# Batch normalisation on one core: four parameter vectors loaded as rows by ScalarE's queue and turned onto the partitions by VectorE

## Chip, cores, metric

One core of a Trainium2 chip. The time is device microseconds of one execution; "before" and "changed" are compared by the medians of their runs.

## The reference

```python
# x: (32, 256, 128, 128) float32; the four parameters: (256,) float32
def reference(x, gamma, beta, running_mean, running_var):
    eps = 1e-5
    mean = running_mean.reshape(1, -1, 1, 1)   # var, gamma, beta likewise
    # ...
    return gamma * (x - mean) / np.sqrt(var + eps) + beta
```

The input and the output are 537 MB each. The parameters are 1 KB each.

## The kernel before

The kernel puts channels on the 128 partitions. A tile is 128 channels of one image: 128 x 16384 floats, 64 KB on each partition, 8.39 MB in all; there are 64 of them and room for three. All large transfers go through SyncE's queue. Per tile VectorE does one multiply-add in place, with a scale and a shift per partition.

```python
NBUF = 3
# ...
    for i in range(NBUF):
        issue_load(i)                      # nc.sync.dma_start, 8.39 MB each

    def load_param(ap_1d):                 # channel j*128 + p goes to partition p, column j
        t = params.tile([P, NCB], mybir.dt.float32, tag=ap_1d.tensor.name)
        nc.gpsimd.dma_start(out=t, in_=ap_1d.rearrange("(j p) -> p j", p=P))
        return t

    var_t = load_param(running_var)        # ... gamma, beta, running_mean
    # ... scale = gamma / sqrt(var + eps), shift = beta - mean * scale, on 128x2
    K = NBUF - 1
    for b in range((NT + K - 1) // K):
        idxs = [i for i in range(K * b, K * b + K) if i < NT]
        for i in idxs:
            compute(i)                     # one multiply-add of 128x16384
        for i in idxs:
            store(i)                       # nc.sync.dma_start
        for i in idxs:
            issue_load(i + NBUF)
```

A parameter load in this form is 256 pieces of 4 bytes, because neighbouring channels lie on different partitions.

## Time and profile before

| Quantity | Value | Where it is read |
|---|---|---|
| Median of the three runs known at the prediction | 2491.8 us (2489.7 to 2493.3) | the runs |
| Mean rate of the transfers | 432 GB/s | page |
| VectorE busy | 23% | page |
| First multiply-add starts | 25.56 us | timeline |
| Store 0 issued, landed | 34.40 us, 82.9 us | timeline, chain |

First, the page of the kernel before. The digits are the busy share of the DMA engines in 40 slices, in tenths, and GB/s is what they moved in each; a line of the queue table gives packets, MB and the share of 16 engines' span.

```profile
DMA  9999999999999999999999999999999999999998
GB/s 414 429 438 433 433 429 437 436 430 431 435 436 433 428 437 436 434 428 436 433 437 428 435 435 435 426 437 436 435 427 435 436 438 426 434 437 436 432 431 378
...
q1 hardware_dynamic: 18432, 1073.75, 99.8%
q0 software_dynamic: 128, 0.00, 0.0%
```

The DMA engines have no free slice, so the time is bytes over rate. The rate is near the ceiling of 435 GB/s (bytes through the 16 ports of SBUF, the core's memory in which the tiles lie) that the Trainium skill, "DMA: Bandwidth & Descriptors", section "Where 436 GB/s comes from", gives for 16 engines, and the trace agrees with it: its packet records show a steady median of 2.418 us for a 64 KB packet, which is 27.1 GB/s per engine and 434 GB/s for 16. The same section says that between HBM (the chip's main memory) and SBUF a lower limit binds, some 358 GB/s per core; this program, on one core, moved 432 GB/s, so here the measurement decides. The parameters' queue has 128 packets and next to no share.

The start decides what the parameters can cost. This is the timeline of the kernel before: start in us, duration in us, engine and line, and in brackets the idle time before it and what ended it.

```profile
0.74 1.33 SPq L48 DMA_DIRECT2D t<-in_x_dram  x3
...
1.25 0.84 POOL L56 DMA_DIRECT2D t<-in_running_var_dram  x1 [0.81 <-PEq L133]
...
12.44 1.28 ACT L71 ACT_TABLE_LOAD   x1 [12.44 <-DMA t<-in_running_var_dram]
...
17.42 0.16 DVE L79 TENSOR_TENSOR scale_t<-t,tmp_t 128x2 f32<-128x2 f32 x1 [3.20 <-DMA t<-in_gamma_dram]
25.17 0.16 DVE L80 TENSOR_TENSOR tmp_t<-t,scale_t 128x2 f32<-128x2 f32 x1 [7.58 <-DMA t<-in_running_mean_dram]
...
25.56 8.81 DVE L86 TENSOR_SCALAR t<-t,scale_t,shift_t 128x16384 f32<-128x16384 f32 x1
34.40 19.06 SPq L97 DMA_DIRECT2D out_dram<-t  x2
44.28 8.81 DVE L86 TENSOR_SCALAR t<-t,scale_t,shift_t 128x16384 f32<-128x16384 f32 x1 [9.91 <-DMA t<-in_x_dram]
63.64 8.81 DVE L86 TENSOR_SCALAR t<-t,scale_t,shift_t 128x16384 f32<-128x16384 f32 x1 [10.55 <-DMA t<-in_x_dram]
82.93 0.34 SPq L48 DMA_DIRECT2D t<-in_x_dram  x1
```

The first multiply-add is released by running_mean at 25 us. But the store of its tile, issued at 34.40 us, waits in the same queue behind loads 1 and 2, whose multiply-adds can start only at 44.28 and 63.64 us. The merged chain of waits (start, duration, what ran) shows the next link:

```profile
34.40 48.51 DMA out_dram<-t
...
82.93 38.59 DMA t<-in_x_dram
```

Store 0 takes 48.5 us from issue to landing, though a tile needs only some 19.3 us of the DMA engines; the rest is time in the queue. The chain follows the multiply-add back to the parameters, but that piece of chain has slack that the view does not show: an earlier issue of store 0 would only wait longer in the queue.

The group of multiply-adds, with busy time, mean of one, and idle time before them:

```profile
L86 DVE TENSOR_SCALAR t<-t,scale_t,shift_t 128x16384 f32<-128x16384 f32 x64 | 564.0, 8812 | 1868.0 <-DMA t<-in_x_dram 1867.9
```

VectorE spends its idle time waiting for tiles.

### The profile page before, as it was taken

The numbers are of one execution on the slowest core, as the hardware profiler recorded it, in microseconds if no ns is written. First come the engines' busy times: TensorE is split into PE (matmuls) and PEld (weight loads), VectorE is DVE, ScalarE is ACT, GpSimd is POOL, SyncE is SP. The second block draws the span as 40 slices with busy tenths as digits, with TensorE's granted clock in tenths as the row PEclk, the third lists the DMA queues.
The fourth block names the chain that finished last, engine by engine and source line by source line (L and its number), as shares of the span: only waits on it lengthen the run. The fifth ranks groups of instructions, "written<-read, shape, count | busy, mean of one in ns | idle before, by whom it ended". The sixth has DMA issues, their size and how long they took to land.

```text
span 2488.1 us, 378 instructions
## 1 busy us (share of the span) xinstructions
DVE 564.7 (23%) x69; ACT 1.6 (0%) x2; POOL 3.2 (0%) x8
## 2 busy tenths in 40 slices
DVE  2122211222112221122212222121221212212121
ACT  0000000000000000000000000000000000000000
POOL 0000000000000000000000000000000000000000
DMA  9999999999999999999999999999999999999998
GB/s 414 429 438 433 433 429 437 436 430 431 435 436 433 428 437 436 434 428 436 433 437 428 435 435 435 426 437 436 435 427 435 436 438 426 434 437 436 432 431 378
DMA packets 18562, 1073.77 MB, mean 432 GB/s; under 512 B 2176, under 2 KB 2176, under 8 KB 2176
## 3 DMA queue, kind: packets, MB, share of 16 engines
q1 hardware_dynamic: 18432, 1073.75, 99.8%
q0 software_dynamic: 128, 0.00, 0.0%
q14 instruction: 2, 0.02, 0.0%
HBM read 536.88 MB, written 536.87 MB: 432 GB/s over the span
## 4 chain that ended last, share of the span: by engine, by line
DMA 51%; another core or an unknown queue 36%; DVE 11%; SPq 0%; issue 0%; POOL 0%; DVEq 0%; POOLq 0%; PEldq 0%
DMA t<-in_x_dram 48%; DVE t L86 11%; DMA out_dram<-t 2%; DMA t<-in_running_mean_dram 1%; SPq L97 0%; POOL t L56 0%; DVEq L86 0%; POOLq L133 0%; SPq L48 0%; DVE shift_t L81 0%; DVE tmp_t L80 0%; DVEq L80 0%; PEldq L133 0%
## 5 line engine op out<-in xcount | busy, mean ns | idle before, releaser
L86 DVE TENSOR_SCALAR t<-t,scale_t,shift_t 128x16384 f32<-128x16384 f32 x64 | 564.0, 8812 | 1868.0 <-DMA t<-in_x_dram 1867.9
L78 DVE RECIPROCAL tmp_t<-tmp_t 128x2 f32<-128x2 f32 x1 | 0.2, 166 | 13.2 <-ACT tmp_t L71 13.2
L80 DVE TENSOR_TENSOR tmp_t<-t,scale_t 128x2 f32<-128x2 f32 x1 | 0.2, 160 | 7.6 <-DMA t<-in_running_mean_dram 7.6
L71 ACT ACT_TABLE_LOAD x1 | 1.3, 1283 | 12.4 <-DMA t<-in_running_var_dram 12.4
L79 DVE TENSOR_TENSOR scale_t<-t,tmp_t 128x2 f32<-128x2 f32 x1 | 0.2, 160 | 3.2 <-DMA t<-in_gamma_dram 3.2
L56 POOL DMA_DIRECT2D t<-in_running_var_dram x1 | 0.8, 839 | 0.8 <-PEq L133 0.8
L56 POOL DMA_DIRECT2D t<-in_gamma_dram x1 | 0.7, 722 | 0.0
L56 POOL DMA_DIRECT2D t<-in_beta_dram x1 | 0.7, 722 | 0.0
L56 POOL DMA_DIRECT2D t<-in_running_mean_dram x1 | 0.7, 722 | 0.0
L71 ACT ACTIVATE tmp_t<-t,eps_t 128x2 f32<-128x2 f32 x1 | 0.3, 295 | 0.0
L65 DVE MEMSET eps_t<- 128x1 f32 x1 | 0.1, 59 | 0.8 <-PEq L122 0.8
L81 DVE TENSOR_TENSOR shift_t<-t,tmp_t 128x2 f32<-128x2 f32 x1 | 0.2, 160 | 0.0
L122 POOL MEMSET const-bfloat16-1.0<- 128x1 bf16 x1 | 0.1, 96 | 0.0
L122 POOL MEMSET const-uint8-127<- 128x1 uint8 x1 | 0.1, 94 | 0.0
L122 POOL MEMSET const-float32-0.0<- 128x1 f32 x1 | 0.1, 93 | 0.2 <-issue 0.2
L122 POOL MEMSET const-float32-1.0<- 128x1 f32 x1 | 0.1, 93 | 0.0
## 6 DMA issues: line engine op xcount, KB each, us to landing
t<-in_x_dram SPq DMA_DIRECT2D x64, 38.6
out_dram<-t SPq DMA_DIRECT2D x64, 49.9
t<-in_running_var_dram POOLq DMA_DIRECT2D x1, 1.0 KB, 11.1
t<-in_gamma_dram POOLq DMA_DIRECT2D x1, 1.0 KB, 15.2
t<-in_beta_dram POOLq DMA_DIRECT2D x1, 1.0 KB, 19.5
t<-in_running_mean_dram POOLq DMA_DIRECT2D x1, 1.0 KB, 21.6
```

Source lines behind the costliest of these rows:

```text
L56: nc.gpsimd.dma_start(out=t, in_=ap_1d.rearrange("(j p) -> p j", p=P))
L65: nc.vector.memset(eps_t, eps)
L71: nc.scalar.activation(out=tmp_t[:], in_=var_t[:], func=mybir.ActivationFunctionType.Sqrt, bias=eps_t[:], scale=1.0,)
L78: nc.vector.reciprocal(out=tmp_t[:], in_=tmp_t[:])
L79: nc.vector.tensor_mul(out=scale_t[:], in0=gamma_t[:], in1=tmp_t[:])
L80: nc.vector.tensor_mul(out=tmp_t[:], in0=mean_t[:], in1=scale_t[:])
L81: nc.vector.tensor_sub(out=shift_t[:], in0=beta_t[:], in1=tmp_t[:])
L86: nc.vector.tensor_scalar(out=t[:], in0=t[:], scalar1=scale_t[:, cb : cb + 1], scalar2=shift_t[:, cb : cb + 1], op0=mybir.AluOpType.mult, ...
L122: nc = _bacc.Bacc("TRN2", target_bir_lowering=False, num_devices=1)
```

## The change

The intent is to replace the four scattered loads by four contiguous rows, take GpSimd out of the kernel, and have the parameters earlier. The order of tiles and transfers on SyncE's queue is kept. VectorE turns 32x32 blocks and four copies move the pieces onto the 128 partitions. The changed kernel also has the line `ctx.enter_context(tc.manual_schedule())`, which the cut below leaves out.

```diff
-    def load_param(ap_1d):
-        t = params.tile([P, NCB], mybir.dt.float32, tag=ap_1d.tensor.name)
-        nc.gpsimd.dma_start(out=t, in_=ap_1d.rearrange("(j p) -> p j", p=P))
-        return t
+    rows = params.tile([B, C], f32, tag="rows")              # B = 32, C = 256
+    nc.vector.memset(rows, 0.0)
+    for r, ap in enumerate((running_var, gamma, beta, running_mean)):
+        nc.scalar.dma_start(out=rows[r : r + 1, :], in_=ap.rearrange("(o c) -> o c", o=1))
 # ... the three first loads of x follow here ...
+    turned = params.tile([B, C], f32, tag="turned")
+    nc.vector.transpose(out=turned[:], in_=rows[:])
+    par = params.tile([P, NCB, 4], f32, tag="par")
+    blocks = turned.rearrange("p (cb q r) -> p cb q r", cb=NCB, q=NQ)   # NQ = 4
+    for q in range(NQ):
+        nc.vector.tensor_copy(out=par[q * B : (q + 1) * B], in_=blocks[:, :, q, 0:4])
+    var_t, gamma_t, beta_t, mean_t = (par[:, :, r] for r in range(4))
 # ... the loop over tiles is rewritten with the same order of computes, stores and loads ...
```

More of the change, by code (lines that the diff above doesn't have):

```diff
@@ L7 @@
 from concourse._compat import with_exitstack
-SINGLE_QUEUE = True
 NBUF = 3
+GROUPS = [2] * 32
+AHEAD = 1
 @with_exitstack
@@ L26 @@
     eps = 1e-5
+    f32 = mybir.dt.float32
     N, C, H, W = x.shape
@@ L33 @@
     NT = N * NCB
+    B = 32
+    NQ = P // B
+    assert sum(GROUPS) == NT and max(GROUPS) <= NBUF
     params = ctx.enter_context(tc.tile_pool(name="params", bufs=1))
@@ L39, with load @@
     outr = out.rearrange("n (cb p) h w -> (n cb) p (h w)", p=P)
+    ctx.enter_context(tc.manual_schedule())
     tiles = {}
-    loads = {}
-    def issue_load(i):
-        if i >= NT:
-            return
-        t = data.tile([P, HW], mybir.dt.float32, tag="t")
-        loads[i] = nc.sync.dma_start(out=t[:], in_=xr[i])
-        tiles[i] = t
-    for i in range(NBUF):
-        issue_load(i)
-    def load_param(ap_1d):
-        t = params.tile([P, NCB], mybir.dt.float32, tag=ap_1d.tensor.name)
-        nc.gpsimd.dma_start(out=t, in_=ap_1d.rearrange("(j p) -> p j", p=P))
-        return t
-    var_t = load_param(running_var)
-    gamma_t = load_param(gamma)
-    beta_t = load_param(beta)
-    mean_t = load_param(running_mean)
-    eps_t = params.tile([P, 1], mybir.dt.float32, tag="eps")
-    nc.vector.memset(eps_t, eps)
-    scale_t = params.tile([P, NCB], mybir.dt.float32, tag="scale")
-    shift_t = params.tile([P, NCB], mybir.dt.float32, tag="shift")
-    tmp_t = params.tile([P, NCB], mybir.dt.float32, tag="tmp")
+    def load(i):
+        t = data.tile([P, HW], f32, tag="t")
+        nc.sync.dma_start(out=t[:], in_=xr[i])
+        tiles[i] = t
+    rows = params.tile([B, C], f32, tag="rows")
+    nc.vector.memset(rows, 0.0)
+    for r, ap in enumerate((running_var, gamma, beta, running_mean)):
+        nc.scalar.dma_start(out=rows[r : r + 1, :], in_=ap.rearrange("(o c) -> o c", o=1))
+    for i in range(AHEAD + GROUPS[0]):
+        load(i)
+    eps_t = params.tile([P, 1], f32, tag="eps")
+    nc.vector.memset(eps_t, eps)
+    turned = params.tile([B, C], f32, tag="turned")
[5 more added lines that the diff above has]
+    var_t, gamma_t, beta_t, mean_t = (par[:, :, r] for r in range(4))
+    scale_t = params.tile([P, NCB], f32, tag="scale")
+    shift_t = params.tile([P, NCB], f32, tag="shift")
+    tmp_t = params.tile([P, NCB], f32, tag="tmp")
     nc.scalar.activation(
         out=tmp_t[:],
-        in_=var_t[:],
+        in_=var_t,
         func=mybir.ActivationFunctionType.Sqrt,
@@ L78 @@
     nc.vector.reciprocal(out=tmp_t[:], in_=tmp_t[:])
-    nc.vector.tensor_mul(out=scale_t[:], in0=gamma_t[:], in1=tmp_t[:])
-    nc.vector.tensor_mul(out=tmp_t[:], in0=mean_t[:], in1=scale_t[:])
-    nc.vector.tensor_sub(out=shift_t[:], in0=beta_t[:], in1=tmp_t[:])
+    nc.vector.tensor_mul(out=scale_t[:], in0=gamma_t, in1=tmp_t[:])
+    nc.vector.tensor_mul(out=tmp_t[:], in0=mean_t, in1=scale_t[:])
+    nc.vector.tensor_sub(out=shift_t[:], in0=beta_t, in1=tmp_t[:])
     def compute(i):
@@ L96, in store @@
         t = tiles.pop(i)
-        (nc.sync if SINGLE_QUEUE else nc.scalar).dma_start(out=outr[i], in_=t[:])
-    K = NBUF - 1
-    for b in range((NT + K - 1) // K):
-        idxs = [i for i in range(K * b, K * b + K) if i < NT]
+        nc.sync.dma_start(out=outr[i], in_=t[:])
+    first = 0
+    for g, size in enumerate(GROUPS):
+        idxs = range(first, first + size)
         for i in idxs:
@@ L105 @@
             store(i)
-        for i in idxs:
-            issue_load(i + NBUF)
+        first += size
+        more = GROUPS[g + 1] if g + 1 < len(GROUPS) else 0
+        for i in range(first + AHEAD, min(first + AHEAD + more, NT)):
+            load(i)
 _INS = ['x', 'gamma', 'beta', 'running_mean', 'running_var']
```

## The prediction

> **What bounds the kernel now.** The transfers. The queue table gives SyncE's queue 99.8% of 16 engines' span, at 432 GB/s; the slices show 9 tenths of DMA throughout. The Trainium skill, "DMA: Bandwidth & Descriptors", section "Where 436 GB/s comes from", puts the ceiling at 435 GB/s; the slices (426 to 438) agree: the steady state has nothing to give. VectorE is busy 23% (64 multiply-adds of 8.81 us) and is covered by other tiles' packets.
>
> **The start.** The timeline shows three loads issued from 0.74 us and four parameter loads on GpSimd's queue at 1.25 to 4.24 us. These land at about 12.4, 17.3, 22.3 and 25.1 us, mostly 4.9 us apart, two 64 KB packets of 2.42 us: each takes a data turn and a semaphore turn among an engine's bulk packets. The skill's section "Queues, rings and completion order" says that an engine goes round its queues packet by packet; this trace agrees. The first multiply-add starts at 25.56 us, released by running_mean. Tile 0's last data packet ended at 24.3 us, so only about 1 us is waited for parameters.
>
> **Is that wait critical? No.** Store 0 is issued at 34.40 us, but stands behind loads 1 and 2, which hold the engines to about 63 us (tile 2's multiply-add starts at 63.64 us). It lands at 82.9 us. Slack: about 29 us. Parameters up to 28 us later, or any earlier, should be invisible.
>
> **What the change does.** The order of SyncE's 128 transfers and of the multiply-adds is the same; waits added on its queue are for transfers long landed. Removed: four GpSimd loads of 4-byte pieces. Their 128 packets took 0.86 us per engine in sum (the first 64 bytes up to 1.0 us, most later ones 25 ns), and bulk packets beside them were slowed (mean 2.62 us at 7 to 10 us, 2.45 us until 25 us, against 2.42 us): estimated 0.5 us more. Added: four ScalarE issues (estimated 0.35 us each, as SyncE's), a memset, a transpose and four copies, estimated under 2 us in all (small operations here take 0.06 to 0.17 us). The table load (1.28 us) no longer waits for the variance. Rows still take turns with bulk packets; I expect all four landed between 8 and 24 us and the first multiply-add at 23 to 26.5 us. Tiles move in SBUF by about 2 KB; I expect nothing of that.
>
> **Sum.** About 1 us less DMA work, 0.04%, below the spread of the three runs (2489.7 to 2493.3). Predicted 2490.8 us, range 2486.5 to 2494.5. Faster by over 2%: 0.5%; within 2%: 99%; slower by over 2%: 0.5%.
>
> **What would show it.** Right: mean rate 431 to 434 GB/s; the software queue's packets vanish and a second hardware queue has some 0.00 MB; store 0 lands at 81 to 83 us; two tiles still take 77.3 us; multiply-adds stay 8.81 us; GpSimd's busy time falls from 3.2 to about 0.4 us. Wrong: bulk packets not 2.42 us (tile addresses matter), longer multiply-adds, or a first multiply-add after some 53 us (rows held behind SyncE's loads), which would leave the engines without work at 63 us.
>
> **What could break it.** Rows starved behind SyncE's queued 25 MB: served only after it, at about 63 us, with some 11 us of small work and a multiply-add to follow, engines would idle some 11 us, still only 0.4%. Larger: a bulk rate that depends on the new SBUF offsets, where 1% is worth 25 us.

## More of the kernel before

The kernels ran in four sets: first before and changed, then three sets of experiments, each of these on another chip. Kernels of one set share their runs of the kernel before, and comparisons across sets are marked.

## The result, and the profile after

| | Before | Changed |
|---|---|---|
| Median | 2490.76 us (2485.85 to 2493.40, 6 runs) | 2486.57 us (2485.91 to 2488.46, 6 runs) |
| Ratio, 95% interval | 1 | 0.999 (0.9979 to 1.0001) |
| First multiply-add starts | 25.56 us | 24.91 us |
| Store 0 landed | 82.9 us | 81.9 us |

A ratio is the mean time of one kernel's fast runs over that of the other's of the same rounds, so not quite the ratio of the medians. The verdict is the same time: the interval contains 1.

The page of the changed kernel, with the lines that answer to those of before:

```profile
DMA  9999999999999999999999999999999999999999
GB/s 420 424 439 434 427 437 438 425 437 437 433 430 436 437 425 436 438 433 430 439 434 427 439 435 432 434 437 434 430 438 435 430 437 435 435 431 437 435 428 397
...
q1 hardware_dynamic: 18432, 1073.75, 99.9%
...
q10 hardware_dynamic: 8, 0.00, 0.0%
```

The parameters now make 8 packets in place of 128. The packet records of the trace show 1 KB and 4 bytes for each row, one after the other, so a row lies on one engine alone.

The timeline of the changed kernel:

```profile
0.73 1.33 SPq L51 DMA_DIRECT2D t<-in_x_dram  x3
...
1.14 0.50 ACTq L58 DMA_DIRECT2D rows<-in_running_var_dram  x1
...
2.21 0.30 ACTq L58 DMA_DIRECT2D rows<-in_running_mean_dram  x1
2.54 1.28 ACT L78 ACT_TABLE_LOAD   x1 [2.54 <-issue]
22.60 0.43 DVE L66 STREAM_TRANSPOSE turned<-rows 32x256 f32<-32x256 f32 x1 [21.48 <-DMA rows<-in_running_mean_dram]
23.07 0.69 DVE L71 COPY par<-turned 32x8 f32<-32x8 f32 x4
...
24.91 8.81 DVE L93 TENSOR_SCALAR t<-t,scale_t,shift_t 128x16384 f32<-128x16384 f32 x1
33.75 17.49 SPq L104 DMA_DIRECT2D out_dram<-t  x2
42.05 8.81 DVE L93 TENSOR_SCALAR t<-t,scale_t,shift_t 128x16384 f32<-128x16384 f32 x1 [8.33 <-DMA t<-in_x_dram]
62.53 8.81 DVE L93 TENSOR_SCALAR t<-t,scale_t,shift_t 128x16384 f32<-128x16384 f32 x1 [11.66 <-DMA t<-in_x_dram]
81.96 0.34 SPq L51 DMA_DIRECT2D t<-in_x_dram  x1
```

Rows are issued by 2.5 us but they land at 7.8, 12.7, 17.6 and 22.5 us: each needs two turns, one for data and one for the semaphore (the count by which its landing is made known), between bulk packets of 2.42 us. So four rows need about eight turns. The turning, copying and square root then cost 2.3 us before the first multiply-add, and it starts only 0.65 us earlier than before. Tile 1 is ready 2.2 us earlier (42.05 against 44.28), tile 2 only 1.1 us (62.53 against 63.64).

The chain of waits after, at the same place:

```profile
33.75 48.15 DMA out_dram<-t
...
81.96 38.59 DMA t<-in_x_dram
```

Store 0 is issued 0.65 us earlier and waits about as long as before. The multiply-adds, where the tiles' new addresses would show, have not changed by a nanosecond in the mean:

```profile
L93 DVE TENSOR_SCALAR t<-t,scale_t,shift_t 128x16384 f32<-128x16384 f32 x64 | 564.0, 8812 | 1864.4 <-DMA t<-in_x_dram 1864.4
```

The two profiled spans are 2488.1 and 2484.1 us, 4.0 us apart. Of these about 1 us is there when store 0 lands. The other 3 us come later, where both kernels move the same packets in the same order; the experiments below ask whether they are real.

### The profile page after: what moved, and what is told of

Its sections match the earlier page's. It is cut to its first block, busy times and chain, and to the rows that moved or that the text cites. A ratio compares the mean times of both kernels' runs of the same rounds, so it can differ in the third digit from the quotient of the medians.

```text
span 2484.1 us, 384 instructions
## 1 busy us (share of the span) xinstructions
DVE 566.0 (23%) x75; ACT 1.6 (0%) x2; POOL 0.2 (0%) x4
## 4 chain that ended last, share of the span: by engine, by line
DMA 51%; another core or an unknown queue 36%; DVE 11%; SPq 0%; issue 0%; DVEq 0%; ACTq 0%; ACT 0%
DMA t<-in_x_dram 48%; DVE t L93 11%; DMA out_dram<-t 2%; DMA rows<-in_running_mean_dram 1%; SPq L104 0%; DVEq L93 0%; ACTq L58 0%; DVE par L71 0%; SPq L51 0%; DVE turned L66 0%; ACT tmp_t L78 0%; DVE rows L56 0%; DVE tmp_t L85 0%; DVE tmp_t L87 0%
## 5 line engine op out<-in xcount | busy, mean ns | idle before, releaser
L93 DVE TENSOR_SCALAR t<-t,scale_t,shift_t 128x16384 f32<-128x16384 f32 x64 | 564.0, 8812 | 1864.4 <-DMA t<-in_x_dram 1864.4
```

Of the source, the lines that this page charges most:

```text
L93: nc.vector.tensor_scalar(out=t[:], in0=t[:], scalar1=scale_t[:, cb : cb + 1], scalar2=shift_t[:, cb : cb + 1], op0=mybir.AluOpType.mult, ...
```

## The experiments

Three theories. **A**: the only real gain is the transfer work that the 4-byte pieces cost at the start, about 1 us, and the arrival of the parameters has slack. **B**: the earlier arrival counts. **D**: the tiles' new place in SBUF (the first at byte 18720 in place of 16768) speeds up the bulk transfers. Against all of them, **C**: the gap is the scatter of runs.

### Does the arrival of the parameters count?

**No parameter transfers at all** (label no_param_loads). Its output is wrong, which doesn't matter for the time.

```diff
-    for r, ap in enumerate((running_var, gamma, beta, running_mean)):
-        nc.scalar.dma_start(out=rows[r : r + 1, :], in_=ap.rearrange("(o c) -> o c", o=1))
```

> The changed kernel with its four parameter transfers taken out (all four parameters then read as the zeros of the memset, so the result is wrong on purpose). It is the most that any way of loading parameters could give. Theory A (all of the small gain is transfer work of the parameters at the start, the first multiply-add is not critical): 2 to 5 us under before, the same as the changed kernel within 1 us, although the first multiply-add no longer waits for any row but for tile 0 alone (22 to 23 us). Theory B (the wait for the rows is critical after all): 2 to 3 us under the changed kernel, since the multiply-add starts 2 to 3 us earlier. Theory C (scatter of runs): no difference from before clear of the interval.

Measured: 2486.62 us, before 2487.28 us in the same rounds, ratio 1.0001 (0.9987 to 1.0014). Timeline of this kernel:

```profile
22.76 8.81 DVE L91 TENSOR_SCALAR t<-t,scale_t,shift_t 128x16384 f32<-128x16384 f32 x1 [19.34 <-DMA t<-in_x_dram]
31.59 19.61 SPq L102 DMA_DIRECT2D out_dram<-t  x2
...
62.44 8.81 DVE L91 TENSOR_SCALAR t<-t,scale_t,shift_t 128x16384 f32<-128x16384 f32 x1 [11.60 <-DMA t<-in_x_dram]
81.82 0.34 SPq L51 DMA_DIRECT2D t<-in_x_dram  x1
```

The first multiply-add starts 2.15 us earlier than in the changed kernel, and tile 2 and load 3 stand within 0.2 us of where they stood there. Theory B falls: nothing that arrives earlier can be seen. This is also the bound for every way of loading parameters, and the changed kernel, at 2486.57 us in the first set, already is at it as far as runs of different sets can tell. It was expected 2 to 5 us under before; the gap was 0.7 us of medians and nothing in the ratio, so the size of A's gain was put too high.

**Rows first, on SyncE's queue** (label rows_first_on_sync):

```diff
-        nc.scalar.dma_start(out=rows[r : r + 1, :], ...
+        nc.sync.dma_start(out=rows[r : r + 1, :], ...
```

> The changed kernel with the four rows issued on SyncE's queue ahead of the first load of x. The rows should land within some 5 us and the first multiply-add wait for tile 0 alone, but load 0 is issued after the memset and four issues (estimated 0.3 to 0.5 us each), at about 2.3 to 2.8 us in place of 0.73 us. If only the start of the bulk transfers counts: 1 to 2 us over the changed kernel. If the arrival of the rows counts: 1 to 2 us under it.

Measured: 2488.64 us, ratio to before 1.0003 (0.9989 to 1.0017); the unchanged changed kernel in the same rounds had 2486.89 us.

```profile
2.38 1.30 SPq L51 DMA_DIRECT2D t<-in_x_dram  x3
3.48 0.43 DVE L66 STREAM_TRANSPOSE turned<-rows 32x256 f32<-32x256 f32 x1 [2.35 <-DMA rows<-in_running_mean_dram]
...
24.34 8.81 DVE L93 TENSOR_SCALAR t<-t,scale_t,shift_t 128x16384 f32<-128x16384 f32 x1 [18.59 <-DMA t<-in_x_dram]
```

All rows had landed by 3.4 us, 19 us earlier than in the changed kernel, but the first load of x was issued 1.65 us later and the median is 1.75 us higher. This fits what was expected if the start of the bulk transfers counts and the arrival of the rows does not; the time alone does not settle it, since the interval of the ratio contains 1. As a version to use it is no better. No experiment pointed to a version that beats the changed kernel, since even the one without parameter loads doesn't.

**Delays** of the first multiply-add (labels delay_short, delay_middle and delay_long) by 9, 17 and 25 memsets on VectorE:

```diff
+    junk = params.tile([P, 2048], f32, tag="junk")
+    for _ in range(9):                      # 17, 25
+        nc.vector.memset(junk, 0.0)
     def compute(i):
```

> The changed kernel with nine memsets of 128x2048 (estimated 2.1 us each, 19 us in all) on VectorE between the shift and the first multiply-add, which should start at about 44 us. If the slack of the first multiply-add is some 28 us: same as the changed kernel within 2 us. If it is critical: 19 us more.

> The changed kernel with 17 memsets (2.26 us apart in the trace of the shorter delay) before the first multiply-add, which should start at about 63 us, as it did with the columns on ScalarE's queue (63.3 us, 14 us over before). If the late arrival of the parameters explains all of that case: 13 to 17 us over the changed kernel, the engines without work for some 10 us from 62 us, and a similar number of slow bulk packets later. If the small packets on ScalarE's queue left a cost of their own: only about 10 us.

> The same with 25 memsets (estimated 53 us), so that the first multiply-add starts at about 78 us and store 0 is issued at about 87 us, 25 us after the engines run out of loads. If the slack is 28 us: 22 to 28 us over the changed kernel. If the wait were critical from the start: 53 us more. If later stages took up idle time: under 10 us.

| Kernel | First multiply-add | Median | Ratio to before (95%) |
|---|---|---|---|
| changed (label after_again) | 24.99 us | 2486.89 us | 0.9997 (0.9984 to 1.0009) |
| delay_short | 44.82 us | 2486.74 us | 0.9990 (0.9976 to 1.0004) |
| delay_middle | 62.93 us | 2500.60 us | 1.0051 (1.0039 to 1.0064) |
| delay_long | 80.89 us | 2517.32 us | 1.0113 (1.0100 to 1.0127) |

The middle delay shared its rounds with after_again; the short and the long one are of another set, whose kernel before had 2488.01 us. Twenty microseconds of delay are free; 38 us cost 13.7 us over after_again, and 56 us cost 30.6 us over the short delay. So the slack ends between 20 and 38 us, as the 28 us of the prediction have it. The packet records narrow this down: between its last packet of load 2 and its first of store 0 a DMA engine stood idle 11.9 us on average with the middle delay and 29.8 us with the long one. Taken from delays of 37.9 and 55.9 us, both leave a slack of 26 us, two to three less than the prediction worked out. The long delay cost 2.6 us more than the upper end of what was expected: a memset step took 2.26 us where 2.1 us had been estimated, so the multiply-add started 3 us later than planned. In the stretch from 62 to 72 us of the middle delay (columns: stretch, length, then busy time and count of VectorE, ScalarE and GpSimd, clock, DMA share, GB/s) the DMA engines start nothing:

```profile
62.00:72.00 10.00, 10.00 (x3) 0.00 (x0) 0.00 (x0) 1.00 0.00 0
```

### Which part of the change matters: the form or the queue?

**Rows, but on GpSimd's queue** (label rows_on_gpsimd):

```diff
-        nc.scalar.dma_start(out=rows[r : r + 1, :], ...
+        nc.gpsimd.dma_start(out=rows[r : r + 1, :], ...
```

> The changed kernel with the rows issued on GpSimd's queue: the form alone, not the queue. If the cost before lay in the 4-byte pieces: same as the changed kernel within 1 us, about 0.1 us or less per engine of parameter packets. If it lay in the use of GpSimd's software queue: same as before within 1 us. Rows should land at 13 to 26 us.

Measured: 2486.31 us, ratio 0.9998 (0.9986 to 1.0011). The rows landed at 10.8 to 23.2 us, the first sooner than expected. The packet records show 128 small packets again, but in sum 0.08 us per engine, where those of the kernel before took 0.86 us. The median agrees with the changed kernel of the first set to 0.3 us, though before was only 1 us above, too near to decide by time alone.

**The 4-byte columns, but on ScalarE's queue** (label columns_on_scalar):

```diff
-        nc.gpsimd.dma_start(out=t, in_=ap_1d.rearrange("(j p) -> p j", p=P))
+        nc.scalar.dma_start(out=t, in_=ap_1d.rearrange("(j p) -> p j", p=P))
```

> The kernel before with its 4-byte parameter pieces issued on ScalarE's queue: the queue alone, not the form. If the cost lay in the pieces: same as before within 1 us, and some 0.3 to 0.9 us per engine of small packets. If it lay in the software queue: same as the changed kernel within 1 us.

Measured: 2501.68 us, ratio 1.0062 (1.0049 to 1.0075), which neither guess had. The page's queue table and its DMA issues (size, us to landing):

```profile
q10 hardware_dynamic: 1088, 0.00, 0.0%
...
t<-in_running_var_dram ACTq DMA_DIRECT2D x1, 1.0 KB, 42.1
t<-in_gamma_dram ACTq DMA_DIRECT2D x1, 1.0 KB, 61.3
t<-in_beta_dram ACTq DMA_DIRECT2D x1, 1.0 KB, 60.9
t<-in_running_mean_dram ACTq DMA_DIRECT2D x1, 1.0 KB, 60.6
```

There are 1088 packets, which is 4 loads x 16 engines x 17: on this queue each 4-byte piece is a packet of its own (16 per engine, and one for the semaphore), where GpSimd's queue packed 16 of them into one of 64 bytes. Each packet takes a turn between bulk packets: 17 x 2.42 us is 41.1 us, and running_var took 42.1 us. The other three came only when the bulk loads had run out, at about 62 us. That is the late arrival which the prediction named as what could break it, though by the number of turns and not because the queue was held back; it lies beyond the slack:

```profile
63.31 26.26 DVE L86 TENSOR_SCALAR t<-t,scale_t,shift_t 128x16384 f32<-128x16384 f32 x3
72.15 9.06 SPq L97 DMA_DIRECT2D out_dram<-t  x2
```

```profile
62.00:72.00 10.00, 9.17 (x4) 0.00 (x0) 0.00 (x0) 1.00 0.00 0
```

Nothing is started for 10 us, as in the middle delay, which has the same start of the first multiply-add within 0.4 us and no 4-byte pieces at all. In time the two ratios are 1.0051 and 1.0062 (different sets, intervals that overlap), so the late arrival explains most, perhaps all, of the 14 us. An engine's idle stretch is 11.9 us in the middle delay and 11.4 us here, and the medians lie some 2 and 3 us higher than that. The packet records of the two have 263 and 450 bulk packets over 2.5 us after 62 us, not the similar numbers that were expected, against 105 to 191 in the eight kernels that were neither late nor had extra loads; but the profiled run of the columns was the slowest of its five (2506.56 us), the long delay has only 178, and what causes these packets is open.

So the move to ScalarE's queue needs the rows, while the rows do as well on GpSimd's queue as on ScalarE's. Moving the loads to ScalarE's queue without making rows of them cost 0.6%: still within 2%, but clear of 1.

### How large is the cost of a parameter load?

It was enlarged by 124 further loads behind the four that are used.

**Columns on GpSimd's queue** (label columns_x32), the kernel before with:

```diff
+    extra = params.tile([P, 124, NCB], mybir.dt.float32, tag="extra")
+    for k in range(124):
+        ap = (running_var, gamma, beta, running_mean)[k % 4]
+        nc.gpsimd.dma_start(out=extra[:, k], in_=ap.rearrange("(j p) -> p j", p=P))
```

> The kernel before with 124 further parameter loads on GpSimd's queue behind the four that are used. Theory A: from the trace of before, a later load costs an engine some 0.03 to 0.15 us in its own packets and about 0.05 to 0.1 us in slowed bulk packets; 124 of them make 10 to 25 us over before. If the loads cost nothing on the engines (scatter alone explains the gap): within 3 us of before.

Measured: 2499.81 us, ratio 1.0047 (1.0033 to 1.0060). In means that is 11.6 us for 124 loads, or 0.093 us each, at the low end of the expectation.

**Rows on ScalarE's queue** (label rows_x32), the changed kernel with, after the square root:

```diff
+    extra = params.tile([B, 2, C], f32, tag="extra")
+    for k in range(124):
+        ap = (running_var, gamma, beta, running_mean)[k % 4]
+        r, j = divmod(k % 62, 2)
+        nc.scalar.dma_start(out=extra[r : r + 1, j, :], in_=ap.rearrange("(o c) -> o c", o=1))
```

> The changed kernel with 124 further row loads on ScalarE's queue, after the square root is issued, so that nothing waits for them. Each row took 46 + 9 ns on one engine alone in the trace of after; 124 make 6.8 us on that one engine. Theory A: 0 to 7 us over the changed kernel, more than 10 us under the 32-fold columns.

Measured: 2525.11 us, ratio 1.0145 (1.0131 to 1.0159), 37 us over before and far from any expectation. The experiment was faulty. In its trace the transfers of SyncE and of ScalarE name the same eight completion semaphores, and each extra row takes one; so loads 1 and 2 had to wait for rows, and load 1 was issued at 33.6 us. Waits of SyncE's queue in this kernel (total us, times, longest):

```profile
SPq L51 <- DMA extra<-in_gamma_dram: 33.6, 1, 33.6
SPq L51 <- DMA extra<-in_beta_dram: 32.5, 1, 32.5
...
SPq L109 <- DMA extra<-in_running_var_dram: 28.6, 1, 28.6
```

It says nothing of the cost of a row. It does say that small transfers on another queue can hold up large ones by way of a shared semaphore, without any shared data.

**Rows on GpSimd's queue** (label rows_x32_on_gpsimd), which has semaphores of its own (its trace shows other numbers for GpSimd than for SyncE): the rows kernel of rows_on_gpsimd with 124 more such loads.

```diff
+    extra = params.tile([B, 4, C], f32, tag="extra")
+    for k in range(124):
+        ap = (running_var, gamma, beta, running_mean)[k % 4]
+        r, j = divmod(k, 4)
+        nc.gpsimd.dma_start(out=extra[r : r + 1, j, :], in_=ap.rearrange("(o c) -> o c", o=1))
```

> The rows issued on GpSimd's queue, with 124 further row loads behind the four that are used. This repairs the 32-fold rows on ScalarE's queue, whose loads shared completion semaphores with SyncE's loads and held two of these back; GpSimd's queue has semaphores of its own. Against the 32-fold columns (about 12 us over before, 0.1 us each) it compares the form on one queue. If the 4-byte form is what costs: the small packets take 11 + 9 ns per engine and load, 124 of them 2.5 us, so 1 to 4 us over the changed kernel. If the turns of small packets themselves cost, whatever their form: about 12 us, as the columns.

Measured: 2488.20 us, ratio 1.0002 (0.9990 to 1.0015). The mean lies 1.4 us over that of after_again of the same rounds, 0.011 us a load; with that scatter it can't be told from nothing. Both 32-fold kernels have 4096 small packets on the same queue. The packet records differ in two ways: 64 bytes as one piece took a median of 11 ns and as sixteen pieces 25 ns, with a mean of 36 ns; and bulk packets from 62 to 500 us had means of 2.461 us beside columns and 2.427 us beside rows. So it is the 4-byte form that costs, not the number of turns. By the means it costs about eightfold, but the two kernels are of different sets and the smaller cost isn't told from nothing, so the factor itself is not shown.

The use of GpSimd is the same in both. An extra issue that fell into a multiply-add was held until its end: all 11 such issues of the columns ended 0.14 to 0.15 us after it, and all 11 of the rows 0.09 to 0.10 us after it. The Trainium skill, "SBUF — State Buffer", section "SBUF: two separate sides", says that GpSimd can't write descriptors, the orders to the DMA engines, while VectorE works in a mode that takes the port they share; these traces agree. From the columns, where an issue else takes 0.72 us:

```profile
25.05 0.72 POOL L67 DMA_DIRECT2D extra<-in_running_mean_dram  x1 [2.02 <-DMA t<-in_running_mean_dram]
...
25.25 9.02 DVE L91 TENSOR_SCALAR t<-t,scale_t,shift_t 128x16384 f32<-128x16384 f32 x1
29.86 4.55 POOL L67 DMA_DIRECT2D extra<-in_running_var_dram  x1 [4.09 <-DMA extra<-in_running_var_dram]
```

At the columns' 0.093 us each, four columns cost some 0.4 us. The first load of before was dearer (up to 1.0 us in its packets), which brings the sum of before's own small packets to 0.86 us.

### The rivals: place in SBUF, and scatter

**The kernel before with its tiles moved** (label before_tiles_moved) to the addresses of the changed kernel:

```diff
+    pad = params.tile([P, 488], mybir.dt.float32, tag="pad")
+    nc.vector.memset(pad[:, 0:1], 0.0)
```

> The kernel before with an unused pad of 488 floats, which puts the three tiles at the same SBUF addresses as the changed kernel (18720 in place of 16768 bytes). Theory A and C: same as before within 1 us, bulk packets at a median of 2418 ns. Theory D (the address of the tiles is what gave the gain): same as the changed kernel, 3 to 4 us under before, with fewer slow bulk packets.

Measured: 2487.53 us, before 2487.28 us, ratio 1.0002 (0.9990 to 1.0015). The bulk packets have the same median of 2.418 us at both places. Theory D falls.

**The changed kernel again** (label after_again, no edit):

> The changed kernel once more, unedited, for a second estimate of the gap on one chip with the kernel before in the same rounds. In three earlier sets the kernel before had medians of 2490.8, 2487.3 and 2488.0 us, the changed one 2486.6 us once. If the cost of the four parameter loads is 1 to 2 us of transfer time: 0.5 to 2.5 us under before. If the first 4 us gap was scatter alone: within 0.5 us.

Measured: 2486.89 us, before 2487.79 us, ratio 0.9997 (0.9984 to 1.0009). The gap of medians is 0.9 us where it had been 4.2. The kernel before had a median of 2487.3, 2488.0 and 2487.8 us in the three sets of nine runs, each on another chip, with single runs from 2485.8 to 2492.7; the first set's 2490.8 was the highest of its medians. Some 3 us of the first gap did not come back, so they belong to the scatter of the kernel before, whether of runs or of chips. Theory C holds for that part. For the 0.9 us that is left, A is not told apart from C by time.

### Where the earlier start went

In the changed kernel tile 1 is ready 2.2 us earlier, but tile 2 only 1.1 us. The packet records place the loss: at 57.8 to 58.6 us start 16 bulk packets of 3.2 to 4.1 us in place of 2.42; they overlap, so one on each engine, and are the last of load 2, just ahead of the first store. The kernel before has none over 2.44 us there. The middle and the long delay, which had no store queued by then, have none over 2.43 us between 30 and 62 us, and the short delay, which had one queued at 53.5 us, has the 16 slow packets again. All seven kernels made from the changed one that had a store queued by then have them (the 32-fold rows on ScalarE's queue, whose loads were held back, aside). So in these kernels the slow packets come with the first turn from loading to storing. They don't come from the parameters: the kernel without parameter loads has the same 16 at 58.0 to 58.5 us. Nor from the tiles' place: the kernel before with its tiles moved has none, like before itself. What else differs, the rewritten loop and the manual schedule, was not tried. Later on the kernel before has such packets too, a few at a time, in clusters some multiple of about 77.4 us apart.

## Why the prediction was right

- **"The transfers" bound the kernel, and the steady state has nothing to give.** Right: 432 GB/s before and after, and no way of loading parameters, not even none at all, went below 2486 us in the median.
- **The wait for parameters is not critical, slack about 29 us.** Right, with 26 us measured. Earlier arrival by 19 us (rows first) and an earlier first multiply-add by 2 us (no loads) gave nothing; a delay of 20 us cost nothing; 38 us cost 13.7 us.
- **Rows land between 8 and 24 us, the first multiply-add at 23 to 26.5 us.** Right but for the first row, which landed at 7.8 us: the last landed at 22.5 us and the multiply-add started at 24.91 us. They take turns with bulk packets, which the Trainium skill, "DMA: Bandwidth & Descriptors", section "Queues, rings and completion order" states and both traces agree with.
- **"About 1 us less DMA work".** The direction fits and the size can't be told from zero in the time: the last set has 0.9 us of medians, with an interval that holds 1. The form of the load is shown to be what costs, by the two 32-fold kernels on GpSimd's queue.
- **2490.8 us.** The measured 2486.57 us is 0.07 us inside the lower end of the range. The term that was off is the starting point: three runs of before at 2491.8 us were taken as its level, and its later sets are at 2487.3 to 2488.0 us. The predicted gain of 1 us fits the 0.9 us of the last set; the base was some 4 us high. That the number still fell inside its range is luck.
- **The tiles' new place costs nothing.** Right: multiply-adds 8812 ns in both, bulk packets 2.418 us in both, and the moved kernel the same as before.
- **Rows starved behind SyncE's loads would idle the engines 11 us.** It did not happen to the rows. The columns on ScalarE's queue made it happen: 11.4 us of idle, 14 us in time.
- Of the smaller signs, GpSimd's busy time fell from 3.2 to 0.2 us, where about 0.4 us was predicted.
- Not foreseen: that a row lies on one engine alone, that each 4-byte piece takes a turn of its own on ScalarE's queue, and that half of the earlier start is lost at the first turn to storing.

## What to carry to other kernels

Before you speed up a setup stage, ask what its last result releases, and whether that would only join a queue that is already full; then a delay put in on purpose measures the slack for the price of one run. When small loads share the engines with large packets, count their turns: in these traces the time to landing was about the turns times the large packet's time, and the same scattered load took 17 turns on ScalarE's queue and 2 on GpSimd's. Take the level of the kernel before from as many runs as you need for the difference that you mean to call.

## What the Trainium skill lacked or had wrong

- "DMA: Bandwidth & Descriptors", section "Queues, rings and completion order", says that an engine drains a packet of typically 9 to 17 descriptors from one ring before it turns to the next. For 4-byte pieces that depends on the queue: GpSimd's packed 16 pieces into one packet (128 packets for four loads), ScalarE's made one packet of each (1088 packets), and with bulk packets of 2.42 us the first load took 42.1 us to land in place of 11.1 us. The page doesn't say so.
- The same page, section "Why a DMA increments its semaphore by 16 and not by 1", takes the number of engines from the slowest dimension that is not 1, as the instruction carries it, and says that software can split a contiguous row. The traces agree: ScalarE's instruction carried a row of 1 x 256 as one element of 1024 bytes and ran on one engine (8 packets for four rows), GpSimd's carried the same row as 16 elements of 64 bytes and ran on all 16 (128 packets). What no page says is that the same line of code is split on one queue and not on the other.
- No page gives the cost of a small packet by its form beside full-rate traffic: 64 bytes took 11 ns as one piece and 25 ns as sixteen (medians), and 46 ns for a 1 KB row.
- No page tells of slow bulk packets where a queue first turns from loads to stores, as in the changed kernel: up to 4.1 us in place of 2.42 us, 16 packets at once.
